# The first value projection of a bidirectional hybrid layer, computed from the scaled input before its norm and shift are known

## The chip, the cores and the metric

The kernel runs on one core of a Trainium2 chip. The metric is the device time of one execution in microseconds; the kernel before took 2884.38 us (median of 3 runs, 2880.95 to 2885.03). One execution was recorded with the hardware profiler. Lower is better.

The names of the engines in the rows: PE is the matrix engine (TensorE), DVE is VectorE, ACT is ScalarE, POOL is GpSimd, and SP is the engine whose queue issues most of the DMA transfers.

## The reference

One layer of a backbone is applied to 640 tokens of width D = 2048: 128 context tokens (a prompt with its own conditioning vector) and 512 latent tokens (a sample with another). What matters here is its beginning:

```python
def rmsnorm(x, g):
    y = xf * lax.rsqrt(jnp.mean(xf * xf, -1, keepdims=True) + EPS)
    return (y * g.astype(jnp.float32)).astype(x.dtype)
...
    sh1, sc1, g1, sh2, sc2, g2 = modulation(cond, p['w_mod'], p['b_mod'])   # silu(cond) @ w_mod + b_mod
    u = rmsnorm(x, p['g_pre_mix']) * (1.0 + sc1) + sh1
    mix, new_state = mixer(u, rows, state, p)
...
    q, k, v, o, ig, fg, z, xbc, dt = jnp.split(u @ p['w_in'], _split_points(IN_SIZES), axis=-1)
```

So every projection of the mixer multiplies u by a part of w_in. Per token t, u = x · r(t) · a + sh, where r(t) is the reciprocal root mean square of the token's row, a = g_pre_mix · (1 + sc1) and sh = sh1. The vectors a and sh have one value per feature and conditioning vector (2 of them), and come from two 2048-wide column groups of the matrix w_mod. The value projection v has 1024 columns, the gates (ig, fg, dt) have 48. Behind the projections stand the mLSTM and SSD recurrences, the output projection and the MLP, which make up most of the time and are the same in both kernels.

## The kernel before

**Tiles.** Features lie on the 128 partitions: x is loaded transposed as `xT`, 16 k-tiles of 128 features by 640 tokens. The left and right factors of the precise products are split in two float32r parts: `ah` and `al` hold the high and the low part of u for the 16 k-tiles, `whi` and `wlo` those of a weight block (`split_block`: ACT rounds the block to `whi`, DVE subtracts). Each product is the sum of three matmuls, high·high, low·high and high·low (`mm_a` with the weights stationary, `mm_b` with the tokens stationary).

**The first stage** (lines 295 to 378), which the change rewrites:

- All of `xT` is loaded first (8 transfers, 2 k-tiles each). ACT squares each k-tile; DVE adds the squares up; 25 matmuls with a column of ones (line 317) sum over the features; the power -0.5 is taken on POOL (line 320); five matmuls with a matrix of ones (line 329) spread r(t) over the partitions as `rb`.
- `mod1(k)` computes a and sh of k-tile k. It streams four 512 KB blocks of w_mod (two transfers) and runs 16 float32 matmuls of 32 x 256 (line 346), four at a time in the four 32-column groups of PE. ACT copies the sums out (line 350, `part`), two transposes (line 261, `mod1t`) turn them, and DVE reduces them and writes `a1` and `modT` (lines 262, 354, 355).
- For each k, DVE and ACT build u (line 366), `ah` (line 367) and `al` (line 368), and PE multiplies it: six matmuls into the gates' two PSUM banks `gps` (line 220), and for each second k 30 matmuls into the five banks `vps` of the first 512 columns of v, "chunk v0" (lines 236 to 238).

**Behind it**, ACT copies the gates out (line 429), ACT and DVE copy the five banks of v0 into a value tile (`v_tile`, line 421), and PE goes on with the transposes of the gates (line 437), a step of the later modulation (`mod_step`, line 272: four float32 matmuls) and chunk v1 (`proj_b`). The gates' own long chain on DVE then runs beside v1 and the first query and key projections.

**What sets the order.** The kernel is written as nested calls; a scheduler places the instructions of each engine in a fixed queue, by a simulated timeline, and a pool's number of buffers decides when a load may be issued. All weight and input loads stand in the one queue of SP, which issues in order: a load that waits for its buffer holds those behind it. The weights lie in HBM in the order in which `block_keys` lists them.

## Time and profile before

| | us |
|---|---|
| three timed runs | 2880.95, 2884.38, 2885.03 |
| the profiled execution, its own time | 2880.88 |
| its span in the trace | 2879.2 |
| PE busy | 2829.3 (98%) |
| DVE busy | 1939.3 (67%) |
| ACT busy | 1287.2 (45%) |
| POOL busy | 408.6 (14%) |

The profiled execution took 1.7 us more than its span, and lies at the lower end of the three timed runs. PE's busy time is modelled from pipelined matmuls: each matmul's record overlaps that of the next one, so what a matmul takes in a row of many is read from the distance between two starts, not from the mean duration of one. A float32 matmul has two records, a float32r matmul one. PE's granted clock was 0.998 of full speed over the span. The busy shares are means over the whole layer; the change lies in the first 150 us, so the rows below are from there, except for a few prices that only later stages show.

### The profile page before, as it was taken

How to read it: one execution, taken by the hardware profiler on the slowest of the kernel's cores; microseconds unless marked ns; L12 is line 12 of the kernel's file. 1: busy time of each engine (PE TensorE's matmuls, PEld its weight loads, DVE VectorE, ACT ScalarE, POOL GpSimd, SP SyncE). 2: the span in 40 equal slices, each digit the busy share in tenths (PEclk: the TensorE clock that was granted, in tenths of full speed). 3: DMA queues.
4: the chain of work that ended last, by engine and by line, in shares of the span. 5: the costliest groups of instructions: out<-in, count | busy, mean ns of one | idle time of the engine just before them, and what ended most of it. 6: DMA issues, size and time to landing. Idle time of an engine off the chain costs nothing.

```text
span 2879.2 us, 48401 instructions
## 1 busy us (share of the span) xinstructions
PE 2829.3 (98%) x18882; PEld 2631.5 (91%) x18882; DVE 1939.3 (67%) x3121; ACT 1287.2 (45%) x2315; POOL 408.6 (14%) x454
## 2 busy tenths in 40 slices
PE   7999999999999999999999999999999999999998
PEld 5679898888887889998999999999999999999997
DVE  4463465787665757678777666666776676677976
ACT  3222333334413433565444444444565566465364
POOL 0000000223211000000000000000014444443200
PEclk9999999999999999999999999999999999999999
DMA  9743434555647667655444333333448998998254
GB/s 366 288 141 108 138 126 138 176 167 156 210 139 227 233 241 253 215 193 166 161 154 138 116 110 113 109 109 108 163 129 182 207 210 190 197 210 185 89 199 167
DMA packets 211748, 498.52 MB, mean 173 GB/s; under 512 B 22424, under 2 KB 111768, under 8 KB 211008
## 3 DMA queue, kind: packets, MB, share of 16 engines
q1 hardware_dynamic: 153872, 429.38, 43.8%
q0 software_dynamic: 39792, 45.73, 10.0%
q10 hardware_dynamic: 17856, 20.32, 1.9%
q8 instruction: 148, 2.42, 0.3%
q14 instruction: 80, 0.66, 0.1%
HBM read 405.33 MB, written 44.97 MB: 156 GB/s over the span
## 4 chain that ended last, share of the span: by engine, by line
PE 86%; DVE 4%; issue 3%; DMA 3%; POOL 2%; ACT 1%; SPq 0%; DVEq 0%; POOLq 0%; ACTq 0%
PE mm L837 18%; PE mm L835 18%; PE mm L836 18%; PE mm L220 10%; PE mm L236 3%; PE mm L238 3%; PE mm L237 3%; PE tr L272 3%; POOL pc L1244 2%; DVE wlo L963 1%; PE mod L346 1%; PE vps L236 1%; DMA raw<-in_w 1%; PE vps L237 1%; PE vps L238 1%
## 5 line engine op out<-in xcount | busy, mean ns | idle before, releaser
L963 ACT CAST whi<-raw 128x512 fp32r<-128x512 f32 (+1 forms) x659 | 499.1, 766 | 588.4 <-PE mm L836 381.1
L963 DVE TENSOR_TENSOR wlo<-raw,whi 128x512 fp32r<-128x512 f32 (+1 forms) x659 | 574.3, 881 | 248.0 <-ACT whi L963 243.9
L835 PE MATMUL mm<-ah,whi 128*128 128x320 f32 x1536 | 478.4, 312 | 8.3 <-ACT whi L963 8.3
L836 PE MATMUL mm<-al,whi 128*128 128x320 f32 x1536 | 475.7, 310 | 0.0
L837 PE MATMUL mm<-ah,wlo 128*128 128x320 f32 x1536 | 474.6, 310 | 1.0 <-DVE wlo L963 0.6
L207 ACT CAST whi<-raw 128x1024 fp32r<-128x1024 f32 x162 | 169.4, 1047 | 422.4 <-PE mm L238 131.1
L835 PEld LDWEIGHTS mm<-ah,whi 128*128 128x128 f32 x1536 | 288.6, 188 | 18.0 <-ACT whi L963 9.8
L208 DVE TENSOR_TENSOR wlo<-raw,whi 128x1024 fp32r<-128x1024 f32 x162 | 202.2, 1249 | 142.1 <-ACT whi L207 141.1
L837 PEld LDWEIGHTS mm<-ah,wlo 128*128 128x128 f32 x1536 | 288.1, 188 | 6.4 <-issue 4.1
L836 PEld LDWEIGHTS mm<-al,whi 128*128 128x128 f32 x1536 | 288.7, 188 | 4.2 <-issue 4.1
L1244 POOL DMA_DIRECT2D pc<-ev x275 | 238.4, 896 | 368.2 <-ACT ev L1243 357.4
L220 PE MATMUL mm<-ah,whi 128*128 128x256 f32 (+1 forms) x768 | 189.7, 319 | 0.0
L220 PE MATMUL mm<-al,whi 128*128 128x256 f32 (+1 forms) x768 | 188.9, 318 | 0.0
L220 PE MATMUL mm<-ah,wlo 128*128 128x384 f32 (+1 forms) x768 | 185.9, 316 | 0.0
L236 PE MATMUL mm<-whi,ah 128*128 128x512 f32 x400 | 161.7, 405 | 0.0
L238 PE MATMUL mm<-whi,al 128*128 128x512 f32 x400 | 159.6, 399 | 0.0
L237 PE MATMUL mm<-wlo,ah 128*128 128x512 f32 x400 | 159.4, 399 | 0.0
L837 PE MATMUL mm<-q,wlo 128*128 128x320 f32 x512 | 157.9, 308 | 0.0
L835 PE MATMUL mm<-q,whi 128*128 128x320 f32 x512 | 157.9, 308 | 0.0
L1243 ACT COPY ev<-mm 128x320 f32<-128x320 f32 x275 | 115.7, 425 | 63.2 <-DMA pc<-ev 45.3
L220 PEld LDWEIGHTS mm<-ah,whi 128*128 128x128 f32 x768 | 121.1, 188 | 10.2 <-issue 9.1
L220 PEld LDWEIGHTS mm<-ah,wlo 128*128 128x128 f32 x768 | 120.7, 188 | 6.9 <-issue 5.8
(424 smaller groups left out, 6680.2 us busy)
## 6 DMA issues: line engine op xcount, KB each, us to landing
raw<-in_w SPq DMA_DIRECT2D x460, 512.0 KB, 3.4
mraw<-in_w SPq DMA_DIRECT2D x128, 512.0 KB, 4.3
pc<-ev POOLq DMA_DIRECT2D x275, 160.0 KB, 5.3
m<-in_w SPq DMA_DIRECT2D x32, 1024.0 KB, 6.6
R<-hd SPq DMA_DIRECT2D x32, 640.0 KB, 6.2
xs<-csd SPq DMA_DIRECT2D x40, 256.0 KB, 5.4
hd<-s ACTq DMA_DIRECT2D x62, 160.0 KB, 3.3
hd<-u ACTq DMA_DIRECT2D x62, 160.0 KB, 1.9
```

Source lines behind the costliest of these rows:

```text
L207: S.copy(hi, t)
L208: V.tensor_sub(lo, t, hi)
L220: PE.matmul(ps[h][:, 0:HW[h]], lhsT=w[:, cs_], rhs=a[:, k, HS[h]], start=(k == 0 and i == 0), stop=(k == KT - 1 and i == 2))
L236: PE.matmul(ps[:, :], lhsT=ah[:, k, tok], rhs=hi[:, wc], start=first, stop=False)
L237: PE.matmul(ps[:, :], lhsT=ah[:, k, tok], rhs=lo[:, wc], start=False, stop=False)
L238: PE.matmul(ps[:, :], lhsT=al[:, k, tok], rhs=hi[:, wc], start=False, stop=last)
L835: PE.matmul(ps, lhsT=wh[:, c], rhs=bh[:, k, :], start=(start and k == 0), stop=False)
L836: PE.matmul(ps, lhsT=wh[:, c], rhs=bl[:, k, :], start=False, stop=False)
L837: PE.matmul(ps, lhsT=wl[:, c], rhs=bh[:, k, :], start=False, stop=(stop and k == nk - 1))
L963: newest[:] = S.copy(hi, src), V.tensor_sub(lo, src, hi)
L1243: S.copy(ev, ps)
L1244: G.dma_start(pi[:, j, :], ev, accum_op=OP.add)
```

## The change

Chunk v0 no longer waits for the norm. Since u = x·a·r(t) + sh, v0 is r(t) · (x·a) W + sh W, where W is the block of w_in; the change computes the two parts apart.

- **From scaled x.** `scaled(k)` writes ah and al of x·a (ACT multiplies by a, DVE subtracts), without r(t) and sh; chunk v0's matmuls run on these. After they have used a k-tile, `modulated(k)` replaces it by u as before, for all later projections. `MD` says after which pair p of k-tiles which pairs are replaced; the first four k-tiles after p = 3 and p = 4, the last four after p = 7.
- **The norm at PSUM's exit.** `v_tile` multiplies each bank by rc5 (r of the bank's tokens) and adds the shift's part, in one DVE instruction a bank.
- **The shift's part.** For each k-tile one float32 matmul (line 408) multiplies sh, two values a feature in a 32-wide tile `shT`, by the raw block of 512 columns, each k in one of four 32-column groups of one bank `vsh`; they are written four together after each second pair. At the end ACT copies the bank out, two matmuls with a selecting matrix (line 477) add the four groups and spread the sums over the partitions, and ACT copies them out.
- **The norm** is computed in the middle (`first_norm`, after pair 2): five matmuls for the sums over features instead of 25, then as before.
- **Loads.** x's eight loads are spread over pairs 0 to 2 (`XL`). mod1's blocks are single 512 KB transfers in seven buffers (five of their own and the two of `mraw`), where before four 1 MB tiles were used. The raw blocks of v0 have three buffers in place of two and are kept until the shift's matmul has read them.
- **The gates** are no longer computed within the loop but as an ordinary projection (`proj_a("g", 0)`, 96 matmuls) behind chunk v0 and ahead of chunk v1.

The core of the diff:

```diff
-            for k in range(KT):
-                if k % 2 == 0:
-                    SY.dma_start(xT[:, k:k + 2, :], A["xT"][:, k * T:(k + 2) * T].rearrange("p (a b) -> p a b", b=T))
...
-            def load_m1(k):
-                    w = p0.tile([P, 2, 1024], F32, tag="m1", name="m1", bufs=4)
...
             def mod1(k):
+                for j in range(4):
+                    i = more["m1"] = more.get("m1", -1) + 1
+                    if i % 7 < 2:
+                        w = wp.tile([P, 1024], F32, tag="mraw", name="mraw", bufs=2)
+                    else:
+                        w = p0.tile([P, 1024], F32, tag="m1", name="m1", bufs=5)
+                    SY.dma_start(w, A["w"][BLK["m1", k, j]])
...
+                V.tensor_copy(shT[:, k, 0:2], modT[:, k, :])
...
+            def scaled(k):
+                for ci, cc in enumerate(CC):
+                    S.activation(ah[:, k, cc], xT[:, k, cc], AF.Copy, scale=a1[:, k, ci:ci + 1])
+                    V.scalar_tensor_tensor(al[:, k, cc], xT[:, k, cc], a1[:, k, ci:ci + 1], ah[:, k, cc],
+                                           OP.mult, OP.subtract)
...
-                mm_a(gps, k, gw[0], gw[1])
...
+            XL = {0: (1, 2), 1: (3, 4, 5), 2: (6, 7)}
+            MD = {3: (0,), 4: (1,), 5: (2, 3), 6: (4, 5), 7: (6, 7)}
+            raws = {}
+            for p in range(KT // 2):
+                raws[p] = raw_block(("B", "v", 0, p))
+                vw = split_block(None, raws[p])
+                if p == 0:
+                    mod1(1)
+                for i in XL.get(p, ()):
+                    load_x(i)
+                if p + 1 < KT // 2:
+                    mod1(2 * p + 2)
+                    mod1(2 * p + 3)
+                for k in (2 * p, 2 * p + 1):
+                    scaled(k)
+                for i in ((0,) if p == 0 else ()) + XL.get(p, ()):
+                    squares(i)
                 for kk in range(2):
+                    k = 2 * p + kk
                     for t in range(NT):
-                        mm_b(vps[t], t, k - 1 + kk, vw[0], vw[1], kk, k - 1 + kk == 0, k - 1 + kk == KT - 1)
+                        mm_b(vps[t], t, k, vw[0], vw[1], kk, k == 0, k == KT - 1)
+                if p % 2:
+                    for g in range(4):
+                        k = 2 * p - 2 + g
+                        PE.matmul(vsh[32 * g:32 * g + 32, :], lhsT=shT[:, k, :],
+                                  rhs=raws[k // 2][:, k % 2 * 512:(k % 2 + 1) * 512], start=(p == 1), stop=(p == 7))
+                if p == 2:
+                    first_norm()
+                for i in MD.get(p, ()):
+                    for k in (2 * i, 2 * i + 1):
+                        modulated(k)
...
+                if shift:
+                    V.scalar_tensor_tensor(o, i, rc5[:, t:t + 1],
+                                           shift[t > 0][:, 0:512].rearrange("p (h e) -> p h e", h=2), OP.mult, OP.add)
...
+        part, shift = fmt(), []
+        S.copy(part[:, 0:512], vsh)
+        for c in range(2):
+            sel = gp.tile([P, P], F32, tag="vsel", name="vsel", bufs=2)
+            V.tensor_scalar(sel, ones, vcol[:, c:c + 1], None, OP.mult)
+            ps = pva()
+            PE.matmul(ps, lhsT=sel, rhs=part[:, 0:512], start=True, stop=True)
+            shift.append(fmt())
+            S.copy(shift[c][:, 0:512], ps)
+        vts = [v_tile(vps, shift)]
...
+        for i, ps in enumerate(proj_a("g", 0)):
+            S.copy(gT[:, HS[i]], ps[0:48, 0:HW[i]])
```

How the change moves instructions on the engines is shown at three places. `m1`, `m` and `mraw` are blocks of w_mod for mod1, `raw` are blocks of w_in; the numbers behind `m` and `part` are buffers, in order of use.

The queue of SP at the start of the program, before:

```order
L111 DMA par<-in_par 128x377
L113 DMA row<-in_row 128x96
L303 DMA xT<-in_xT 128x1280 x8
L337 DMA m_213<-in_w 128x2x1024
L337 DMA m_215<-in_w 128x2x1024
L337 DMA m_243<-in_w 128x2x1024
L337 DMA m_245<-in_w 128x2x1024
```

The same place in the changed program, from its first block of w_mod on:

```order
L323 DMA mraw<-in_w 128x1024 x2
L323 DMA m_120<-in_w 128x1024
L323 DMA m_122<-in_w 128x1024
L340 DMA xT<-in_xT 128x1280
L199 DMA raw<-in_w 128x1024
L323 DMA m_164<-in_w 128x1024
L323 DMA m_166<-in_w 128x1024
L323 DMA m_168<-in_w 128x1024
L323 DMA mraw<-in_w 128x1024
L340 DMA xT<-in_xT 128x1280 x2
```

The blocks of the first k-tile now come ahead of x, and the eight transfers of x stand among blocks of w_mod and w_in: the last of them, x's k-tiles 14 and 15, has 11 blocks of w_mod, 3 of w_in and the 7 other transfers of x ahead of it.

PE in the middle of the loop, before, from one mod1's transposes to the next product of the gates:

```order
L261 MATMUL mod1t<-ident,part_392 128x128 x2
L346 MATMUL mod_418<-m_414,scT 32x256 x8
L236 MATMUL vps<-whi,ah 128x512
L237 MATMUL vps<-wlo,ah 128x512
L346 MATMUL mod_418<-m_416,scT 32x256 x8
L238 MATMUL vps<-whi,al 128x512
L220 MATMUL gps<-ah,whi 128x384
L220 MATMUL gps<-ah,whi 128x256
```

PE in the middle of the loop of the changed program, from the last high products of one k-tile of v0 to mod1 of the next but one:

```order
L235 MATMUL vps<-whi,ah 128x512
L236 MATMUL vps<-wlo,ah 128x512
L408 MATMUL vsh<-raw,shT 32x512
L237 MATMUL vps<-whi,al 128x512 x5
L260 MATMUL mod1t<-ident,part_645 128x128 x2
L328 MATMUL mod_663<-mraw,scT 32x256 x4
L328 MATMUL mod_663<-m_657,scT 32x256 x4
L328 MATMUL mod_663<-m_659,scT 32x256 x4
L328 MATMUL mod_663<-m_661,scT 32x256 x4
```

The gates' matmuls have left the loop. The shift's matmuls, written four together in the source, stand one by one, one in each k-tile's stretch, with float32r matmuls of the full width on both sides; mod1's 16 matmuls stand together behind the transposes.

ACT behind chunk v0 in the changed program (`fm` are scratch tiles; the cast in the third row is of a block of chunk v1):

```order
L374 ACTIVATE ah<-u,modT 128x128
L374 ACTIVATE ah<-u,modT 128x512
L206 CAST whi<-raw 128x1024
L472 COPY fm<-vsh 128x512
L514 ACTIVATE arow<-row 128x32
L479 COPY fm<-pva 128x512 x2
L206 CAST whi<-raw 128x1024 x2
```

PE at the same place:

```order
L237 MATMUL vps<-whi,al 128x512 x5
L477 MATMUL pva<-fm,vsel 128x512 x2
L271 MATMUL tr<-mraw,scT 32x256 x4
L219 MATMUL mm<-ah,whi 128x384
L219 MATMUL mm<-ah,whi 128x256
```

Before, the gates' copies (line 429) and the copies of the five banks stood at this place of ACT, and on PE the gates' transposes followed v0's last matmuls directly. Now the shift's copy stands behind a cast that needs the buffer of v0's last weight block, PE's two selecting matmuls wait for that copy, and the gates' 96 matmuls come between v0 and v1.

## Rows read from the trace of the kernel before

**Rows 1.** The page: span, PE's busy time and the engines' shares of the chain of waits.

```profile
span 2879.2 us, 48401 instructions
...
PE 2829.3 (98%) x18882; PEld 2631.5 (91%) x18882; DVE 1939.3 (67%) x3121; ACT 1287.2 (45%) x2315; POOL 408.6 (14%) x454
...
PE 86%; DVE 4%; issue 3%; DMA 3%; POOL 2%; ACT 1%; SPq 0%; DVEq 0%; POOLq 0%; ACTq 0%
```

**Rows 2.** Busy time of the engines in stretches of 20 us: stretch, length, PE, PEld, DVE, ACT, POOL (busy us and number of instructions), PE's granted clock, busy share of the DMA engines, GB/s.

```profile
0.00:20.00 20.00, 2.62 (x12) 2.57 (x12) 10.45 (x21) 12.32 (x18) 1.20 (x8) 1.00 0.87 332
20.00:40.00 20.00, 19.73 (x133) 15.87 (x133) 6.07 (x14) 4.89 (x10) 1.18 (x1) 1.00 1.00 394
40.00:60.00 20.00, 19.32 (x159) 12.34 (x158) 10.03 (x23) 6.36 (x11) 0.00 (x0) 1.00 1.01 397
...
120.00:140.00 20.00, 18.69 (x168) 12.33 (x165) 9.77 (x23) 6.89 (x12) 0.00 (x0) 1.00 0.53 194
...
160.00:180.00 20.00, 20.00 (x103) 14.77 (x101) 11.03 (x31) 3.16 (x6) 0.00 (x0) 1.00 0.38 133
```

**Rows 3.** For whom PE waited in the first 150 us: who, for whom, total us, times, longest.

```profile
PE nrm L317 <- ACT sq L305: 15.6, 1, 15.6
PE mod L346 <- DVE sm L262: 2.6, 9, 0.5
...
PE ms L437 <- ACT v L421: 1.0, 1, 1.0
```

**Rows 4.** PE's timeline from the start: start, length, line, operation, tiles, count of records, idle before.

```profile
17.94 4.42 PE L317 MATMUL nrm<-ones,sq 128*128 128x1 f32 x20 [15.57 <-ACT sq L305]
22.23 2.27 PE L317 MATMUL nrm<-ones,rb 128*128 128x1 f32 x10
24.36 4.41 PE L317 MATMUL nrm<-ones,sq 128*128 128x1 f32 x20
28.69 3.64 PE L346 MATMUL mod<-m,scT 128*32 128x256 f32 x32
32.26 2.40 PE L329 MATMUL nrm<-rb,ones 128*128 128x128 f32 x10
34.50 0.38 PE L261 MATMUL mod1t<-ident,part 128*128 128x128 f32 x2
35.15 1.93 PE L346 MATMUL mod<-m,scT 128*32 128x256 f32 x32 [0.27 <-DVE sm L262]
37.02 0.50 PE L236 MATMUL vps<-whi,ah 128*128 128x512 f32 x1
```

**Rows 5.** PE's timeline in the loop: one k-tile from transposes to transposes.

```profile
48.45 0.38 PE L261 MATMUL mod1t<-ident,part 128*128 128x128 f32 x2
...
55.92 0.38 PE L261 MATMUL mod1t<-ident,part 128*128 128x128 f32 x2
56.56 1.07 PE L346 MATMUL mod<-m,scT 128*32 128x256 f32 x16 [0.27 <-DVE sm L262]
...
63.35 0.38 PE L261 MATMUL mod1t<-ident,part 128*128 128x128 f32 x2
```

**Rows 6.** PE's timeline behind the first stage: the last product of v0, the gates' transposes, a mod_step, and chunk v1's first products up to the next mod_step.

```profile
146.53 1.09 PE L238 MATMUL vps<-whi,al 128*128 128x512 f32 x4
148.66 0.51 PE L437 MATMUL ms<-ident,fm 48*128 48x48 f32 x5 [1.04 <-ACT v L421]
149.10 0.64 PE L272 MATMUL tr<-mraw,scT 128*32 128x256 f32 x8
149.67 0.50 PE L236 MATMUL mm<-whi,ah 128*128 128x512 f32 x1
150.01 0.40 PE L237 MATMUL mm<-wlo,ah 128*128 128x512 f32 x1
...
156.75 0.64 PE L272 MATMUL tr<-mraw,scT 128*32 128x256 f32 x8
```

**Rows 7.** PE's timeline in a later stage: two float32 matmuls of 257 columns between float32r matmuls.

```profile
282.02 0.60 PE L658 MATMUL ms<-St,qw 128*128 128x257 f32 x2
282.45 0.60 PE L659 MATMUL ms<-v,pT 128*128 128x257 f32 x2
282.70 0.65 PE L220 MATMUL mm<-ah,wlo 128*128 128x384 f32 x2
```

**Rows 8.** The chain of waits, in order of time (start, length, what): 48 matmuls of a projection of the gates' form, one weight block.

```profile
223.22 7.08 PE mm L220 x48
```

**Rows 9.** ACT's timeline: the squares of x's first and last transfer, each started when the transfer had landed.

```profile
7.61 0.74 ACT L305 ACTIVATE rb<-xT 128x640 f32<-128x640 f32 x1 [4.11 <-DMA xT<-in_xT]
...
18.73 1.36 ACT L305 ACTIVATE sq<-xT 128x640 f32<-128x640 f32 x2 [0.22 <-DMA xT<-in_xT]
```

**Rows 10.** Groups of instructions of DVE and ACT in the first 152 us: line, engine, operation, tiles and shapes, count, busy us, mean ns of one, idle before.

```profile
L368 DVE SCALAR_TENSOR_TENSOR al<-u,modT,ah 128x512 fp32r<-128x512 f32 x16 | 12.0, 750 | 5.8 <-ACT ah L367 5.8
...
L309 DVE TENSOR_TENSOR rb<-rb,sq 128x640 f32<-128x640 f32 x11 | 9.1, 825 | 6.1 <-ACT sq L305 5.0
...
L421 DVE COPY v<-vps 128x512 f32<-128x512 f32 x2 | 1.2, 647 | 0.0
...
L207 ACT CAST whi<-raw 128x1024 fp32r<-128x1024 f32 x13 | 13.6, 1043 | 25.4 <-PE vps L238 20.4 <-PE gps L220 5.0
...
L421 ACT COPY v<-vps 128x512 f32<-128x512 f32 x3 | 1.7, 587 | 0.1
```

More of the change, by code (lines that the diff above doesn't have):

```diff
@@ L311, in build @@
-            pt = pv.tile([P, 512], F32, tag="g", name="nrm", bufs=2)
-            parts = [late[KT - 4], late[KT - 3], rb, late[KT - 2], late[KT - 1]]
-            V.memset(rc5, 0.0)
-            PE.matmul(pt[:, 0:NT], lhsT=ident, rhs=rc5, start=True, stop=False)
-            for n, x in enumerate(parts):
-                for i in range(NT):
-                    PE.matmul(pt[:, i:i + 1], lhsT=x[:, i * P:(i + 1) * P], rhs=ones[:, 0:1],
-                              start=False, stop=n == 4 and i == NT - 1)
@@ L332, in load_m1 @@
[L332 to L342 removed]
+            shT = p0.tile([P, KT, 32], F32, name="shT")
+            V.memset(shT, 0.0)
@@ new lines, in load_x, with squares, first_norm @@
+            def load_x(p):
+                SY.dma_start(xT[:, 2 * p:2 * p + 2, :],
+                             A["xT"][:, 2 * p * T:(2 * p + 2) * T].rearrange("p (a b) -> p a b", b=T))
+            def squares(p):
+                for k in (2 * p, 2 * p + 1):
+                    sq = tmp("sq") if k else rb
+                    S.activation(sq, xT[:, k, :], AF.Square)
+                    if k:
+                        V.tensor_add(rb, rb, sq)
+            def first_norm():
+                pt = pva()
+                for i in range(NT):
+                    PE.matmul(pt[:, i:i + 1], lhsT=rb[:, i * P:(i + 1) * P], rhs=ones[:, 0:1], start=True, stop=True)
+                V.tensor_scalar(rc5, pt[:, 0:NT], 1.0 / D, EPS, OP.mult, OP.add)
+                G.tensor_tensor(rc5, rc5, mhalf[:, 0:NT], OP.pow)
+                for i in range(NT):
+                    V.tensor_scalar(rb[:, i * P:(i + 1) * P], ident, rc5[:, i:i + 1], None, OP.mult)
+                for c in (slice(0, 512), slice(512, T)):
+                    pt = pva()
+                    for i in range(c.start, c.stop, P):
+                        PE.matmul(pt[:, i - c.start:i - c.start + P], lhsT=ones, rhs=rb[:, i:i + P], start=True, stop=True)
+                    S.copy(rb[:, c], pt[:, 0:c.stop - c.start])
```

84 lines of the change are left out of this document (30 added, 54 removed).

## The prediction

> **What bounds the kernel now.** I read the page first: PE is busy for 2829.3 of 2879.2 us and takes 86% of the chain of waits [rows 1]. So a stage gains only what PE is spared in it, and what PE loses is not made up later: from 160 us on PE is busy 20.00 us in 20 [rows 2]. Next, the stretches of the first stage. In the first 20 us PE works 2.6 us while the loads run at 332 GB/s; from 20 to 60 us both are full (PE 19.3 to 19.7 of 20, DMA share 1.00, 394 to 397 GB/s); towards the end the loads fall to 0.53 and PE stays at 18.7 [rows 2]. So before, the stage is bound by the load of x at its head and by PE behind it, with the loads close below. The waits say the same: PE's one long wait is 15.6 us for the squares of x; all others together are 5 us [rows 3]. On the timeline that head has three parts: nothing until 17.94, then 25 slow norm matmuls until 28.69 (10.75 us, 0.43 each), then mod1 [rows 4].
>
> The mark by which I measure is the start of chunk v1 on PE: 149.67 us before, with the gates done and five gate transposes (148.66 to 149.10, 0.44 us) and one mod_step (0.57 us) ahead of it [rows 6].
>
> **The start of the changed program: when PE stops waiting for loads.** x arrives at (18.73 - 7.61) / 7 = 1.59 us for each 655,360 bytes [rows 9]; a block of 524,288 bytes then takes 0.8 of that, 1.27 us, and the stream begins at 7.61 - 1.59 = 6.0 us. The changed queue of SP puts 11 blocks of w_mod, 3 of w_in and 7 other transfers ahead of x's last. It lands at 6.0 + 14 x 1.27 + 8 x 1.59 = 36.5 us, where before the last landed at 18.7. Until then PE can do mod1 of k-tiles 0 to 2 and v0 of k-tiles 0 and 1, some 14 us of work in 30: it starves, because x stands in the way of w_mod. Then come two squares (1.36 us, rows 9), an addition of 0.83 us [rows 10] and five norm matmuls (5 x 0.43 = 2.2 us, rows 4). PE's queue holds the transposes of k-tile 2 behind those, so they run at about 41.1 us. Before, they ran at 48.45 [rows 5], with the same v0 work and two k-tiles of the gates done. So the twenty norm matmuls saved (8.6 us) and the early start leave a lead of 7 us here, not of 28.
>
> **The loop from there, for PE.** One k-tile's stretch in the changed order is: transposes and the wait for DVE's reduction until mod1 may take the bank, 0.64 us [rows 5]; mod1's 16 matmuls together, 35.15 to 37.02, 1.87 us [rows 4]; 15 matmuls of v0, by the spacing of v1's 30 (149.67 to 156.75, 0.236 each, rows 6), 3.54 us; and one matmul of the shift.
>
> The shift's matmul is the new price. The nearest rows are two float32 matmuls of 257 columns between float32r ones: the second starts 0.43 us after the first [rows 7]. For 512 columns that makes 0.86. Its weights are 32 columns wide, as in a mod_step, where four of 256 columns take 0.57 us [rows 6] against 0.43 for one, so the change to 32-column groups and back costs 0.14: in all 1.0 us. The upper bound is 1.14 (twice the mod_step). The lower bound is 0.25: mod1's sixteen take 1.87 us, 0.117 for each 256 columns because four run at once, and an alone-standing one would cost that little only if it ran beside its neighbours. I take 1.0, since in the order it stands between matmuls of full width, as in rows 7.
>
> The Trainium skill's page "TensorE: Matmul & The Clock Gate", section "Part 3: Packing small matmuls — row/col tiling", says that matmuls at different column positions run at the same time, so that a pack costs little more than one of them. This case's trace agrees where four stand together: 0.57 us for four of 256 columns. By that rule the source's four matmuls of the shift would cost about 1.0 us together, 0.25 each; the scheduled order has taken the pack apart, and the sum below does not use it.
>
> The sum is 0.64 + 1.87 + 3.54 + 1.0 = 7.05 us. Read the other way: before, the 14 k-tiles from 48.45 to the end of v0 at 147.62 took 7.08 each, gates of 0.88 us included (a sixteenth of two times 7.08, rows 8); with 1.0 in their place that is 7.20. I take 7.1. The loads need 4.5 blocks x 1.27 = 5.7 us for a k-tile, so they keep up. DVE gains one more pair of instructions for each k-tile (0.75 us for the 512 columns, rows 10, and less for the 128) on top of 10 us in 20 [rows 2]: hidden. ACT's share is smaller still.
>
> So the transposes of k-tile 15 run at 41.1 + 13 x 7.1 = 133.4, plus 2.4 us for the norm's five spreading matmuls [rows 4] and 0.6 for a mod1 that the order splits: 136.4. The last k-tile has no mod1 to hide its chain: 2.5 us from transposes to first product (34.50 to 37.02, rows 4), 3.54 and 1.0: v0 ends at 143.5. Before it ended at 147.62.
>
> **Behind v0.** Before, PE waited 1.04 us for the copies [rows 3]. Now a chain of ACT and PE stands there, with nothing else on PE: the cast that is queued ahead of the shift's copy and needs v0's last weight tile (1.04 us, rows 10), the copy (0.59), a selecting matmul (0.87, from rows 7), its copy (0.59), the second matmul in the same single bank (0.87) and its copy (0.59): 4.55, and 0.1 for each handover, 5.1 us. Queued behind the waiting matmul are the mod_step and all gates. It could be as short as 2.5 us, if the cast and the second round are out of the way, and as long as 7. DVE's five instructions at PSUM's exit (0.65 us each as copies, rows 10) run beside the gates; only the first bank's is waited for. Then a mod_step (0.57) and the gates, two weight blocks of 7.08 us [rows 8], 14.2: chunk v1 starts at 143.5 + 5.1 + 14.7 = 163.3. The gates' transposes (0.44), already done before at this mark, come later: 163.8 against 149.67, which is 14.1 us later. The gates leave the loop and come back whole, so they cancel; the delay is the shift's matmuls, the chain behind v0 and the starved start, less the lead of 7 us.
>
> Behind the mark PE's work is the same and PE is full, so the delay stays. The gates' chain starts one block of v1 later; v1 and the first queries cover it as before.
>
> **The number.** The sum is made on the profiled execution: 2880.88 + 14.1 = 2895.0. That execution lies 3.5 us under the median of the runs, which spread over 4.1. I add the 14 to the middle of the three runs, 2883.0: 2897 us. 0.2% of the time, 5.8 us, is about what a measurement can tell from no change.
>
> **Rivals.**
> - *The shift's matmuls run beside their neighbours.* At 0.25 us each, 14 of them in the stretch that PE bounds give 10.5 us back: +3.6, 2887, not to be told from no change. For it speaks the packing of mod1's matmuls; against it that the neighbours use all 128 columns. Chance 0.12.
> - *The early start pays.* PE's 18 idle and 10.75 slow us at the head are real, and the last block of w_mod could land at 6.0 + 72 x 1.27 + 8 x 1.59 = 110 us. If PE followed the loads, v0 would end at about 110 + 1.1 + 7.1 = 118, v1 start at 138.5: -11, 2872. The place is the loop: it decides from a stretch under 7.1 - 14.1 / 13 = 6.0 us on. Against it: the matmuls alone are 6.4. Chance 0.07.
> - *The order of loads holds PE up.* The raw blocks now wait for the shift's matmul of three pairs ago, and blocks of w_mod stand behind them in SP's queue. The shift's matmul ends some 8 us before the next stretch but one begins, and PE needs the block behind it only in that stretch; two blocks land in 3 to 6 us. Should it fail, each of the last four pairs costs about 3 us: +26, 2909. Chance 0.12.
> - The forecast, with its own range of 2890 to 2904: 0.62. What is left, 0.07, is a later stage that the scheduler has rearranged, to either side.
>
> Faster than by 0.2% holds the early start: 0.07. Within 0.2%: the rival of the packed matmuls, 0.12. Slower: 0.81. The range of 2885 to 2910 takes in the bounds of the shift's matmul and of the chain behind v0 and the held-up loads; it leaves the early start out.
>
> **What the profile will show.** First product of v0 before 20 us, but PE under half busy until 40; x's last squares at 36 to 38 us. A period of 7.1 us between two pairs of transposes, with one line 408 matmul after which the next starts 0.9 to 1.1 us later. A gap on PE of 3 to 4 us around the line 477 matmuls near 145 us, ended by ACT. Gates of 14 us, v1 from about 163. I am wrong if the period is near 6, if line 408 takes 0.3 us, or if the delay at v1's start is not that at the end.

## The result, and the profile after

The changed kernel takes 2922.23 us (median of 4 runs, 2919.06 to 2924.19), the kernel before 2884.31 (4 runs, 2880.95 to 2885.03): a ratio of 1.0132, 95% interval 1.0118 to 1.0146, or 38 us more. The forecast was 2897 in a range of 2885 to 2910. Its direction held; its size was too small by 25 us and the range did not hold the time. The profiled execution of the changed kernel took 2920.77 us, that of the kernel before 2880.88, which lies 3.4 us under the median of its runs; so a lag that is read between the two traces ends 2 us above the difference of the medians.

The page after, against [rows 1]:

```profile
span 2919.0 us, 48592 instructions
...
PE 2856.4 (98%) x18876; PEld 2630.1 (90%) x18876; DVE 1959.5 (67%) x3180; ACT 1300.9 (45%) x2346; POOL 411.1 (14%) x454
...
PE 87%; DVE 6%; DMA 4%; issue 2%; ACT 1%; POOL 0%; SPq 0%; DVEq 0%; ACTq 0%; POOLq 0%
```

PE has six records fewer and is busy 27 us longer. The stretches of the first stage after, against [rows 2] (the last three columns are PE's granted clock, DMA share and GB/s):

```profile
0.00:20.00 20.00, 10.09 (x49) 3.20 (x49) 5.51 (x19) 5.16 (x8) 1.20 (x8) 1.00 0.87 321
20.00:40.00 20.00, 14.19 (x86) 6.68 (x85) 15.05 (x22) 13.11 (x20) 0.00 (x0) 0.86 1.02 411
40.00:60.00 20.00, 19.27 (x120) 11.74 (x121) 10.69 (x32) 7.53 (x16) 1.18 (x1) 0.80 0.87 321
120.00:140.00 20.00, 17.66 (x123) 9.85 (x125) 8.61 (x26) 5.80 (x12) 0.00 (x0) 1.00 0.69 252
140.00:160.00 20.00, 15.19 (x80) 7.33 (x70) 14.40 (x36) 9.21 (x16) 1.45 (x2) 0.93 0.38 123
160.00:180.00 20.00, 19.80 (x126) 17.71 (x123) 6.20 (x10) 2.73 (x4) 0.00 (x0) 0.89 0.38 119
```

PE starts earlier and is then emptier: 24.3 us of work in the first 40, against 22.4 before. In four of the six stretches the granted clock is under 1.00, where it reads 1.00 in all of [rows 2]. At the head that reading cannot be taken at its word: up to 34.5 us the kernel before ran its matmuls at half their later pace (mod1's 16 took 32.26 - 28.69 = 3.57 us, and 1.87 from 35.15 on, rows 4), and so did the changed kernel up to about 21 us (eight records of mod1 take 0.94 us from 20.03 on and 0.46 from 23.49 on). The waits of PE up to 160 us, against [rows 3]:

```profile
PE mod L328 <- DVE sm L261: 9.4, 14, 0.8
PE mod L328 <- DMA mraw<-in_w: 7.9, 1, 7.9
PE mod L328 <- DMA m<-in_w: 4.3, 3, 3.9
PE vps L235 <- ACT ah L366: 2.5, 2, 1.7
PE pva L477 <- ACT fm L472: 1.7, 1, 1.7
...
PE pva L477 <- ACT fm L479: 0.7, 1, 0.7
PE tr L271 <- ACT fm L479: 0.7, 1, 0.7
```

The first line is the surprise: 2.6 us in 9 times before, now 9.4 in 14, up to 0.8 each. PE's head, against [rows 4]:

```profile
33.65 1.07 PE L328 MATMUL mod<-m,scT 128*32 128x256 f32 x16
38.58 1.08 PE L328 MATMUL mod<-m,scT 128*32 128x256 f32 x8 [3.87 <-DMA m<-in_w]
40.20 2.29 PE L353 MATMUL pva<-ones,rb 128*128 128x1 f32 x10 [0.53 <-DVE rb L348]
42.35 0.67 PE L260 MATMUL mod1t<-ident,part 128*128 128x128 f32 x2
```

One k-tile of the loop on PE, against [rows 5], and DVE beside it:

```profile
105.11 1.04 PE L408 MATMUL vsh<-raw,shT 128*32 128x512 f32 x2
106.09 1.42 PE L237 MATMUL vps<-whi,al 128*128 128x512 f32 x5
107.34 0.38 PE L260 MATMUL mod1t<-ident,part 128*128 128x128 f32 x2
108.50 1.93 PE L328 MATMUL mod<-m,scT 128*32 128x256 f32 x32 [0.78 <-DVE sm L261]
110.37 0.50 PE L235 MATMUL vps<-whi,ah 128*128 128x512 f32 x1
...
115.13 0.38 PE L260 MATMUL mod1t<-ident,part 128*128 128x128 f32 x2
```

```profile
106.69 0.35 DVE L375 SCALAR_TENSOR_TENSOR al<-u,modT,ah 128x128 fp32r<-128x128 f32 x1 [3.66 <-PE vps L237]
107.61 0.75 DVE L375 SCALAR_TENSOR_TENSOR al<-u,modT,ah 128x512 fp32r<-128x512 f32 x1 [0.57 <-PE vps L237]
108.28 0.17 DVE L261 TENSOR_REDUCE sm<-mod1t 128x4 f32<-128x16 f32 x1
```

The period is 115.13 - 107.34 = 7.79 us. The shift's matmul takes 106.09 - 105.11 = 0.98 of it. The reduction `sm`, for which PE's next mod1 waits, stands in DVE's queue behind the low part of a replaced k-tile (line 375), and that waits for PE's last product of the k-tile (line 237). So mod1's matmuls wait 0.78 us behind the transposes, half a microsecond more than the 0.27 of before. Behind v0, against [rows 6]:

```profile
151.99 1.32 PE L237 MATMUL vps<-whi,al 128*128 128x512 f32 x5
155.04 1.13 PE L477 MATMUL pva<-fm,vsel 128*128 128x512 f32 x2 [1.72 <-ACT fm L472]
156.84 1.58 PE L477 MATMUL pva<-fm,vsel 128*128 128x512 f32 x2 [0.68 <-ACT fm L479]
159.09 1.08 PE L271 MATMUL tr<-mraw,scT 128*32 128x256 f32 x8 [0.68 <-ACT fm L479]
...
177.03 0.64 PE L271 MATMUL tr<-mraw,scT 128*32 128x256 f32 x8
177.60 0.50 PE L235 MATMUL mm<-whi,ah 128*128 128x512 f32 x1
```

Chunk v1 starts at 177.60 against 149.67: 27.9 us later. The remaining 10 us of the 38 come behind that mark, in stages that the change does not touch. By the first state matmul of the mLSTM (257.9 before) the lag is 30.8, at the last MLP matmul of line 888 it is 39.9, the 2 us named above included. The granted clock is not the cause there: from v1 to the end it reads 1.00 in both traces.

### The profile page after: what moved, and what is told of

The parts are those of the page before. It is cut to its first block, busy times and chain, and to the rows that moved or that the text cites. A ratio compares the mean times of both kernels' runs of the same rounds, so it can differ in the third digit from the quotient of the medians.

```text
span 2919.0 us, 48592 instructions
## 1 busy us (share of the span) xinstructions
PE 2856.4 (98%) x18876; PEld 2630.1 (90%) x18876; DVE 1959.5 (67%) x3180; ACT 1300.9 (45%) x2346; POOL 411.1 (14%) x454
## 4 chain that ended last, share of the span: by engine, by line
PE 87%; DVE 6%; DMA 4%; issue 2%; ACT 1%; POOL 0%; SPq 0%; DVEq 0%; ACTq 0%; POOLq 0%
PE mm L888 19%; PE mm L890 19%; PE mm L889 19%; PE mm L219 10%; PE mm L235 3%; PE mm L237 3%; PE mm L236 3%; PE tr L271 2%; DMA raw<-in_w 2%; DMA R<-hd 1%; DVE wlo L1016 1%; PE mod L328 1%; DMA xs<-csd 1%; PE vps L235 1%; PE vps L237 1%
## 5 line engine op out<-in xcount | busy, mean ns | idle before, releaser
L888 PEld LDWEIGHTS mm<-ah,whi 128*128 128x128 f32 x1536 | 289.0, 188 | 19.4 <-ACT whi L1016 10.0
L890 PEld LDWEIGHTS mm<-ah,wlo 128*128 128x128 f32 x1536 | 288.4, 188 | 5.7 <-issue 3.7
L889 PEld LDWEIGHTS mm<-al,whi 128*128 128x128 f32 x1536 | 289.0, 188 | 3.0 <-issue 2.9
L219 PE MATMUL mm<-ah,whi 128*128 128x384 f32 (+1 forms) x800 | 199.1, 322 | 0.2 <-DVE v L461 0.2
L219 PE MATMUL mm<-al,whi 128*128 128x384 f32 (+1 forms) x800 | 196.0, 319 | 0.0
L219 PE MATMUL mm<-ah,wlo 128*128 128x384 f32 (+1 forms) x800 | 193.7, 317 | 0.0
L219 PEld LDWEIGHTS mm<-ah,whi 128*128 128x128 f32 x800 | 127.2, 190 | 10.8 <-issue 9.6
L219 PEld LDWEIGHTS mm<-al,whi 128*128 128x128 f32 x800 | 126.8, 190 | 7.4 <-issue 6.2
```

Of the source, the lines that this page charges most:

```text
L219: PE.matmul(ps[h][:, 0:HW[h]], lhsT=w[:, cs_], rhs=a[:, k, HS[h]], start=(k == 0 and i == 0), stop=(k == KT - 1 and i == 2))
L888: PE.matmul(ps, lhsT=wh[:, c], rhs=bh[:, k, :], start=(start and k == 0), stop=False)
L889: PE.matmul(ps, lhsT=wh[:, c], rhs=bl[:, k, :], start=False, stop=False)
L890: PE.matmul(ps, lhsT=wl[:, c], rhs=bh[:, k, :], start=False, stop=(stop and k == nk - 1))
```

## The experiments

18 kernels ran. For each, the table gives the median, the ratio to the kernel before with its interval, the difference to the kernel before run beside it (its medians were 2883.2 to 2885.8), the lag of v1's first matmul in the trace, and the rest, which came behind that mark. The lag is that of one trace, and the first stage alone differs by 1 to 2 us between executions (e12 and e17 start v1 earlier than the kernel before with the same instructions). The last column, a difference of medians less the lag of a trace, is therefore good to some 3 us. The trace of the kernel before is late at v1 and early at the end, so a lag that is read to the end of a trace grows more: by 7.0 us behind v1 in e14, a plain delay, and by 12.0 in the changed kernel. Differences from the changed kernel below are of the medians; with the kernel before of the same run as base they are up to 1.2 us smaller.

| | median us | ratio (95%) | over before | v1's lag | behind v1 |
|---|---|---|---|---|---|
| changed kernel | 2922.2 | 1.0132 (1.0118-1.0146) | 37.9 | 27.9 | 10.0 |
| e1 12 shift matmuls out | 2905.3 | 1.0081 (1.0068-1.0095) | 22.2 | 13.7 | 8.5 |
| e2 shift matmuls together | 2903.5 | 1.0074 (1.0061-1.0088) | 20.3 | 11.0 | 9.3 |
| e3 DVE's order | 2914.1 | 1.0113 (1.0099-1.0126) | 30.9 | 21.2 | 9.7 |
| e4 before, gates later | 2903.7 | 1.0069 (1.0056-1.0081) | 20.5 | 10.6 | 9.9 |
| e5 e4 without two mod_steps | 2899.1 | 1.0050 (1.0037-1.0063) | 14.8 | 10.5 | 4.3 |
| e6 e2 and e3 | 2902.0 | 1.0062 (1.0049-1.0075) | 17.7 | 12.6 | 5.1 |
| e7 x's loads spread | 2913.5 | 1.0102 (1.0086-1.0117) | 29.2 | 18.9 | 10.3 |
| e8 all of these | 2909.7 | 1.0089 (1.0075-1.0103) | 25.4 | 15.1 | 10.3 |
| e9 without two mod_steps | 2924.4 | 1.0133 (1.0119-1.0146) | 38.6 | 27.9 | 10.7 |
| e10 e2 without mod_steps, two banks | 2907.6 | 1.0078 (1.0063-1.0094) | 21.8 | 10.8 | 11.0 |
| e11 filler | 2923.8 | 1.0132 (1.0115-1.0150) | 38.0 | 27.9 | 10.1 |
| e12 before, 64 bytes | 2888.5 | 1.0014 (1.0005-1.0023) | 3.6 | -1.8 | 5.4 |
| e13 e5, 64 bytes | 2905.1 | 1.0073 (1.0061-1.0086) | 20.2 | 9.6 | 10.6 |
| e14 before, plain delay | 2897.8 | 1.0045 (1.0032-1.0059) | 12.9 | 9.9 | 3.0 |
| e15 old places | 2919.5 | 1.0118 (1.0103-1.0133) | 35.7 | 29.4 | 6.3 |
| e16 old places, no mod_steps | 2924.2 | 1.0133 (1.0119-1.0147) | 40.3 | 30.6 | 9.7 |
| e17 before, 32 bytes lower | 2896.6 | 1.0033 (1.0021-1.0046) | 12.7 | -1.2 | 13.9 |
| e18 e16 with e2 | 2902.4 | 1.0058 (1.0045-1.0070) | 18.5 | 11.4 | 7.1 |

None is faster than the kernel before.

**The loop: e1, e2, e3, e6.** e1 leaves out the shift's matmuls of k-tiles 4 to 15 and keeps the first four:

```diff
-                if p % 2:
+                if p == 1:
...
-                                  rhs=raws[k // 2][:, k % 2 * 512:(k % 2 + 1) * 512], start=(p == 1), stop=(p == 7))
+                                  rhs=raws[k // 2][:, k % 2 * 512:(k % 2 + 1) * 512], start=True, stop=True)
```

> The changed kernel with 12 of its 16 shift matmuls left out (only those of k-tiles 0 to 3 stay, so the shift's part of the first value chunk is incomplete). Theory (each shift matmul costs PE about 1.0 us of its own, as the spacing in the changed kernel's loop says): the 12 cost 12 us, chunk v1 starts near 165.5 instead of 177.6, the period between two pairs of transposes is 6.8 instead of 7.78 us, and the time is about 2910. Rival (the period is set by another chain, DVE's or the loads', and the shift's matmuls lie in its slack): the period stays above 7.5, v1 starts after 174, the time is 2918 to 2922.

16.9 us faster than the changed kernel; v1 starts 14.3 earlier (163.32), and the period from k-tile 4 to 15 is 6.6 us in the mean, between 5.5 and 7.2. The rival falls: the matmuls cost 14.3 / 12 = 1.2 us each, together with what they hold up (PE's waits for `sm` fall from 9.4 to 5.9 us). e2 queues the four behind the pair's last product:

```diff
-                        mm_b(vps[t], t, k, vw[0], vw[1], kk, k == 0, k == KT - 1)
+                        last = mm_b(vps[t], t, k, vw[0], vw[1], kk, k == 0, k == KT - 1)
...
+                        with tc.issue_after(last.ins):
+                            PE.matmul(vsh[32 * g:32 * g + 32, :], lhsT=shT[:, k, :],
```

> The changed kernel with the four shift matmuls of two pairs kept together behind the pair's last product. Theory (standing alone is what makes them dear: four in the four column groups run at once, as mod1's do): four take 1.0 to 1.2 us together instead of 4 x 1.0, about 11 us less at the start of v1, time about 2911. Rival (a float32 matmul of 512 columns costs its 1.0 us wherever it stands): no difference, 2922. Second rival (the raw blocks are now held until the end of the pair, and w_mod blocks queue behind the next one): PE waits for loads, 2922 or more with DMA waits in the loop.

PE's timeline of e2, the four (8 records) and what follows:

```profile
111.26 1.06 PE L409 MATMUL vsh<-raw,shT 128*32 128x512 f32 x8
112.25 0.44 PE L260 MATMUL mod1t<-ident,part 128*128 128x128 f32 x2
```

Four take 112.25 - 111.26 = 0.99 us, as long as one alone in the changed kernel. That is what the Trainium skill's page "TensorE: Matmul & The Clock Gate", section "Part 3: Packing small matmuls — row/col tiling", says of matmuls at different column positions, here shown for 512 columns. The gain was 18.7 us and not 11, 16.9 of it at v1. Of that, 12 x 0.98 = 11.8 us are the matmuls, and 2.7 are waits: only 9 of the k-tiles still waited for DVE (6.7 us in all), not 14 (9.4). The other 2.4 are not taken apart. e3 changes DVE's queue alone:

```diff
+                    with tc.issue_after(done[min(k + 1, KT - 1)].ins):
                         V.scalar_tensor_tensor(al[:, k, cc], u[:, cc], modT[:, k, ci:ci + 1], ah[:, k, cc],
```

> The changed kernel with the low part of each replaced k-tile queued on DVE behind the low part of the next scaled k-tile, so that it no longer stands between PE's last product and the reduction of mod1's sums. Theory (DVE's queue holds the reduction behind an instruction that waits for PE itself, 0.5 us for each k-tile from k-tile 4 on): the wait of mod1's matmuls falls from 0.78 to 0.27 us, the period from 7.78 to 7.3, v1 starts 5 to 6 us earlier and the time is about 2916. Rival (something else is late next, ACT or the w_mod blocks): the period stays at 7.7 or more, 2922.

```profile
104.66 0.38 PE L260 MATMUL mod1t<-ident,part 128*128 128x128 f32 x2
105.30 1.93 PE L328 MATMUL mod<-m,scT 128*32 128x256 f32 x32 [0.27 <-DVE sm L261]
...
111.93 0.38 PE L260 MATMUL mod1t<-ident,part 128*128 128x128 f32 x2
```

In this timeline of PE the wait is 0.27 and the period 111.93 - 104.66 = 7.27, as expected; the time is 8.2 us under the changed kernel's. So the half microsecond is DVE's queue.

e6 has the edits of e2 and e3.

> The changed kernel with both: the four shift matmuls together (e2) and the low parts of replaced k-tiles behind the scaled ones on DVE (e3). Theory (two separate losses): e2's period of 6.73 us loses the 0.5 us on those k-tiles where DVE's reduction still stood behind, about 6 us in all, v1 starts near 155 and the time is 2896 to 2899. Rival (the packing took that loss away already, since e2 gained 18.7 us and not 11): 2902 to 2904.

The rival holds: e6 is no faster than e2 (2902.0 and 2903.5), and v1 starts 1.6 us later in it. With the matmuls together, PE waits 6.7 us for the reduction, with DVE's order changed as well 7.3: this order on DVE takes nothing off those waits once the matmuls stand together. Why they remain is not shown.

**The head: e7 and e11.** e7 queues x's loads behind the w_mod blocks and spreads them:

```diff
+                    with tc.issue_after(mdma[2 * p + 2].ins):
+                        for i in XL.get(p, ()):
+                            load_x(i)
...
-            XL = {0: (1, 2), 1: (3, 4, 5), 2: (6, 7)}
-            MD = {3: (0,), 4: (1,), 5: (2, 3), 6: (4, 5), 7: (6, 7)}
+            XL = {0: (1,), 1: (2, 3), 2: (4, 5), 3: (6, 7)}
+            MD = {4: (0, 1), 5: (2, 3), 6: (4, 5), 7: (6, 7)}
```

> The changed kernel with x's loads held behind the w_mod blocks of their pair in SP's queue and spread over pairs 0 to 3, the norm after pair 4 and the replacing from pair 4 on. Theory (the changed kernel starves at its head because the scheduler puts seven x loads ahead of the w_mod blocks of k-tiles 2 and 3): the wait of 7.9 and 4.3 us for w_mod goes, the granted clock stays at full in 20 to 60 us, the transposes of k-tile 2 run near 33 instead of 42.4, the period stays 7.8, v1 starts 7 to 9 us earlier, time 2913 to 2915. Rival (the loads are only moved: the same bytes are missing two or three pairs later): k-tile 2 near 33 but k-tile 9 where it was, time 2920 to 2923. A second one: the replaced k-tiles come so late that the gates wait for DVE, 2922 or more.

The first stretches of e7:

```profile
20.00:40.00 20.00, 17.82 (x128) 9.23 (x126) 9.06 (x17) 7.58 (x12) 0.00 (x0) 1.00 1.03 410
40.00:60.00 20.00, 17.93 (x128) 9.83 (x128) 9.52 (x24) 8.56 (x15) 0.00 (x0) 1.00 1.03 410
```

The transposes of k-tile 2 run at 31.38 instead of 42.35, the clock stays at full, v1 starts 9.0 us earlier and the time is 8.7 lower. The theory holds for the sum, but not for the way there: the lead over the changed kernel is 13.6 us at k-tile 3, 8.5 at k-tile 9 (a period of 8 to 9 us where x's loads and the norm now stand), and 9.9 at k-tile 15.

e11 fills the wait of 3.87 us ahead of k-tile 2's transposes:

```diff
+                    if k == 2 and kk == 12:
+                        dummy = pva()
+                        for _ in range(4):
+                            with tc.issue_after(m.ins):
+                                m = PE.matmul(dummy, lhsT=ones, rhs=xT[:, 0, 0:512], start=True, stop=True)
```

> The changed kernel with four extra float32 matmuls of 512 columns, whose result nobody reads, in PE's queue where it waits 3.9 us for the last w_mod block of k-tile 2 (34.7 to 38.6 us). Theory (the granted clock falls to half behind that wait, and the work until 48.7 us pays for it): with the wait filled the clock stays at full in 38 to 49, k-tile 3's transposes run 2.5 to 4 us earlier than at 53.15, the time is 2918 to 2920. Rival (the clock there costs nothing, since the stretch waits for loads and DVE anyway, or falls all the same): k-tile 3 within 1 us of 53.15, or later by what the extra work costs; 2922 or more.

The granted clock in the changed kernel, in stretches of 2 to 3 us, and then in e11:

```profile
35.00:38.00 3.00, 0.00 (x0) 0.00 (x0) 2.89 (x4) 2.18 (x5) 0.00 (x0) 0.99 1.01 405
38.00:40.00 2.00, 1.08 (x8) 0.20 (x8) 1.79 (x3) 0.99 (x3) 0.00 (x0) 0.50 1.05 418
...
46.00:48.00 2.00, 2.00 (x7) 0.34 (x3) 1.23 (x1) 0.08 (x1) 0.00 (x0) 0.50 1.03 410
48.00:50.00 2.00, 2.00 (x17) 1.29 (x16) 0.00 (x0) 0.00 (x0) 0.00 (x0) 0.96 1.03 410
```

```profile
35.00:38.00 3.00, 1.86 (x5) 0.56 (x3) 2.79 (x3) 2.28 (x4) 0.00 (x0) 1.00 1.02 407
38.00:40.00 2.00, 1.14 (x11) 0.42 (x11) 1.75 (x4) 0.82 (x2) 0.00 (x0) 1.00 1.03 410
...
42.00:44.00 2.00, 2.00 (x4) 0.50 (x2) 1.42 (x6) 0.00 (x0) 0.72 (x1) 0.50 1.04 408
44.00:46.00 2.00, 2.00 (x13) 0.77 (x12) 0.23 (x1) 1.05 (x1) 0.00 (x0) 0.73 1.02 410
```

Between the theories: the stretch at the lower level (1.2 of 2.4 GHz) shrank from ten microseconds to about three and a half, but did not go; k-tile 3's transposes came 2.6 us earlier (50.57; the last block of k-tile 2 was there 0.3 earlier) and k-tile 15's 2.4. Yet v0's last products ran at 151.91, in the changed kernel at 151.99, and the time is the same. PE's timeline of e11 in the last k-tile of v0:

```profile
146.74 0.50 PE L235 MATMUL vps<-whi,ah 128*128 128x512 f32 x1 [2.53 <-ACT ah L372]
...
147.39 1.87 PE L414 MATMUL vsh<-raw,shT 128*32 128x512 f32 x2
149.19 0.80 PE L235 MATMUL vps<-whi,ah 128*128 128x512 f32 x1
```

That k-tile waited 2.5 us for ACT instead of 1.7, and behind the wait the granted clock fell again, to 0.51 from 147.5 to 151 us: the shift's matmul took 149.19 - 147.39 = 1.80 us instead of 0.98. So the clock's price at the head was real, and filling the wait won nothing: what it gave was lost at v0's end, to ACT's `ah` and to the clock.

**The gates: e4, e5, e9.** e4 is the kernel before with this one part of the change: no `mm_a` in the loop, the gates' blocks listed behind v0's, and `proj_a("g", 0)` behind v0 in place of the two copies.

> The kernel before with one part of the change alone: the gates out of the loop, as an ordinary projection behind chunk v0. Theory (the gates' matmuls only move, and what comes behind is the same): v1 starts within 2 us of 149.67 plus the two mod_steps that now stand ahead of it (1.1 us), time 2884 to 2887. Rival (the gates' chain, now one block of v1 later, puts the mLSTM and SSD stages in another order that costs the 10 to 12 us which the changed kernel loses behind v1's start): v1 near 150, but the end 8 to 14 us later, 2893 to 2898.

Both theories miss: 20.5 us. v1 starts 10.6 us later, where I had expected 3 at most. The two blocks of gates are back, 14 us, and two mod_steps; but the loop without them gained only 4.3 by v0's last products (142.27 against 146.53). Its last two k-tiles took (137.53 - 123.85) / 2 = 6.84 us each, against (140.94 - 127.22) / 2 = 6.86 before. Where the gates' products had stood, PE now waits more: 4.0 us for the reduction (before 2.6) and 2.4 for `ah` (before none). That is 3.8 of the 9.9 us that the loop did not give back; the rest I cannot place. And 10 us more came behind v1. e5 leaves the two mod_steps out of the gates' projection:

```diff
-                if mod["n"] < MODCAP[0]:
+                if name != "g" and mod["n"] < MODCAP[0]:
```

> The run with the gates moved alone (e4), but without the two mod_steps that the gates' projection issues as every projection does, so that each later mod_step stands at the block where it stood before. Theory (e4 loses 10 us behind its first mLSTM instructions because every later mod_step comes two blocks earlier and the scheduler arranges the SSD and MLP stages otherwise): the lag against the kernel before stays at 10 to 12 us from the first mLSTM instruction to the end, time 2892 to 2895. Rival (the gates' chain that arrives later does it): the lag grows by 8 to 11 us as in e4, time 2901 to 2905.

2899.1: behind v1 4.3 us are left of 9.9, although PE now waits 1.6 us for v0's banks (in e4 0.9) and 2.1 for v1's behind v1. The intervals of e4 and e5 overlap (1.0056 to 1.0081 and 1.0037 to 1.0063), so the difference is hardly clear of noise. It looked like the theory; e9 is the same edit in the changed kernel.

> The changed kernel without the two mod_steps in the gates' projection, nothing else. Theory (those two steps shift all later ones by two blocks, and the other arrangement of the SSD and MLP stages costs 6 to 9 us, as e4 against e5): v1 starts about 1 us earlier, the lag against the kernel before stays flat from the first mLSTM instruction (near 31) to the end instead of growing by 9 us, time 2913 to 2916. Rival (in the changed kernel the growth comes from its other loads or its longer delay): the lag still ends at 38 to 40, 2920 to 2923.

It fell: 2924.4, with 10.7 us behind v1. From v1 on e9's order on PE is that of e5 but for 46 of 17,074 matmuls. The same order grows by 4 us in one and by 11 in the other.

**Put together: e8, e10.** e8 has e2, e3, e5's edit, e7's and, for the second selecting matmul, a bank of its own; e10 has e2, e5's edit and that bank.

> The changed kernel with all of it: shift matmuls together, DVE's order, x's loads spread (e7), no mod_steps in the gates' projection, and a bank of its own for the second selecting matmul behind v0. Theory (separate losses): 2922 - 18.7 - 5 - 9 - 8 - 1 is 2880, at or below the kernel before. Rival (the losses overlap: each of them hides another, since PE has one queue): 2890 to 2897.

> The changed kernel with the shift matmuls together (e2), no mod_steps in the gates' projection and a second bank for the second selecting matmul. Theory (the losses add here, since they stand in different stretches): 2903.5 - 7 - 1 is 2895 to 2896. Rival (e8's way: arranging one stage anew spoils another): 2902 or more.

e10's rival holds; e8 is slower than even its rival had it (2890 to 2897), so the losses overlap by more than I thought. In e8 PE waits 4.9 us for ACT's `part` and 4.3 for `ah` in the loop, where squares, norm and replaced k-tiles now all stand, behind v0 2.2 us for the shift's last copy and 1.7 for v0's banks, and 1.9 for v1's banks behind v1. e10's six runs spread from 2902.8 to 2914.7, more than any other kernel's.

**Behind v1: e14, e12, e13, e17, e15, e16, e18.** e14 puts 14 unread float32 matmuls into the last k-tile of v0, in the kernel before.

> The kernel before with 14 float32 matmuls of 512 columns, whose result nobody reads, on PE within the last k-tile of chunk v0: a plain delay of 14 x 0.86 = 12 us ahead of v1. Theory (what comes behind v1 only moves): 12 us at v1 and 12 at the end, 2895 to 2898. Rival (any delay of the first stage costs more behind, because the scheduler arranges later stages anew): 12 at v1, 17 to 22 at the end, 2902 to 2906.

12.9 us, as the theory says: the 14 matmuls hold PE for 11.2 us (142.83 to 151.01 and 152.30 to 155.33), v1 starts 9.9 later, since the wait of 1.0 us for v0's banks is gone and the trace is 0.8 quicker up to k-tile 15's transposes. So a plain delay moves what follows and costs 2 or 3 us more at the end. e12 is the kernel before with 64 bytes more of constants; every instruction's place in its queue is the same, one memset aside. The changed kernel has this shift too: `rc5` and `vcol` stand among the constants.

```diff
+        padt = cp.tile([P, 16], F32, name="padt")
+        V.memset(padt, 0.0)
```

> The kernel before with one unused tile of 64 bytes a partition behind its constants, so that every later tile lies 64 bytes higher, as in the changed kernel; no engine's order of instructions differs from the kernel before, apart from one memset. Theory (the drift behind v1's start, which the same order has in e9 and not in e5, comes from where the tiles lie): 6 to 10 us slower, 2890 to 2895. Rival (place has no price): within 3 us of the kernel before.

> e5 (gates later, without their two mod_steps) with the same 64 bytes. Its order behind v1 is e9's but for 46 of 17,074 places, and now its addresses are e9's too. Theory (place): the lag grows behind the first mLSTM instruction by 8 to 11 us as in e9, time 2904 to 2908. Rival (the arrival of data behind the changed first stage): as e5, 2897 to 2901.

> The kernel before with one constant tile of 32 bytes laid into a tile that is no longer used: the weight tiles now begin at multiples of 256 bytes (before: 32 above one; in the changed kernel 96 above one); the order stays. Theory (it is the alignment of the tiles that has a price): 2 to 5 us faster than before, 2880 to 2882. Rival (any other place is worse or as good by chance): 2884 to 2889.

e12 is 3.6 us slower (ratio 1.0005 to 1.0023), between its theory and its rival; e13 is 5.4 slower than e5 against the kernel before, with 10.6 us behind v1 as in e9. e17, 32 bytes lower with every tile of weights at a multiple of 256 bytes, is slower by 12.7 (9.5 by the ratio), more than either of its theories has: place has a price, and it is not alignment in this sense. Where it is paid is harder to say. PE's groups of e17 over the whole program, then those of the kernel before, and then those of e14, whose tiles lie where they lay before (count, busy us, mean ns of one, idle ahead):

```profile
L835 PE MATMUL mm<-ah,whi 128*128 128x320 f32 x1536 | 479.6, 312 | 8.2 <-ACT whi L963 8.2
...
L236 PE MATMUL mm<-whi,ah 128*128 128x512 f32 x400 | 162.7, 407 | 0.0
```

```profile
L835 PE MATMUL mm<-ah,whi 128*128 128x320 f32 x1536 | 478.4, 312 | 8.3 <-ACT whi L963 8.3
...
L236 PE MATMUL mm<-whi,ah 128*128 128x512 f32 x400 | 161.7, 405 | 0.0
```

```profile
L840 PE MATMUL mm<-ah,whi 128*128 128x320 f32 x1536 | 479.4, 312 | 10.3 <-ACT whi L968 10.3
...
L236 PE MATMUL mm<-whi,ah 128*128 128x512 f32 x400 | 161.7, 405 | 0.0
```

e17 is about 1 us longer than the kernel before in each large group of matmuls, 0.3 to 0.8%, and waits 4 us more for DVE's `wlo` in the MLP (7.9 against 3.8). But e14's first group is as long as e17's without any tile having moved, so that part is not the place; the groups of 512 columns and the waits (in e14 3.8 as before) may be. The lag of e17 grows little by little through mLSTM, SSD and the MLP's end, and not at all between 1350 and 2030 us; e14's grows in the same way, by 7.0 us.

e15 lays `rc5` and `vcol` into a constant that is no longer used, in the changed kernel; e16 adds e5's edit, e18 e2 too.

```diff
-        rc5 = cp.tile([P, NT], F32, name="rc5")
+        rc5 = cth[:, 0:NT]
```

> The changed kernel with its two new small constants (rc5, vcol) laid into a constant tile that is no longer used, so that every later tile lies where it lay before the change, 64 bytes lower; the order on all engines stays. Theory (place, as e12's 3.6 and e13's 5.4 us more): 4 to 5 us faster than the changed kernel, 2917 to 2919. Rival (place matters only with before's order): 2921 to 2924.

> e15 and no mod_steps in the gates' projection: the changed first stage, with the order behind v1 and the addresses of e5. Theory (growth behind v1 is place plus order, about 5 us each): the lag grows by 4 us as in e5 instead of 10, time 2915 to 2918 (v1 starts at +28). Rival (a third cause in the changed kernel): the lag grows by 8 or more, 2920 or later.

> The changed kernel with the shift matmuls together, the tiles at their old places and no mod_steps in the gates' projection. Theory (separate causes add): v1 at +11 as in e2, 4 us of growth behind it, 2899 to 2900, the fastest with the changed first stage. Rival (as e10, where the other arrangement spoiled it): 2903 or more.

e15 is 2.7 us faster, less than its runs spread (2914 to 2924): not told apart. e16 has e5's order and places, but 9.7 us behind v1 and not 4: the rival, something in the changed first stage itself, holds, and I cannot name it. e18 is no faster than e2 or e6; only its profiled execution, the lowest of its five, grows by 4.9 us behind v1 as its theory has it.

## Why the prediction was wrong

By its steps, first to v1's start (forecast 163.3, measured 177.6):

- *What bounds the kernel* held, and so did "what PE loses is not made up later".
- *The start* was right in kind: k-tile 2's transposes at 42.35, forecast 41.1. PE starved because x stood ahead of w_mod; e7 gave 9 us back. That the granted clock would fall to half behind such a wait was not in the sum; e11 puts its price at about 2.4 us, which k-tile 15's transposes still show and v0's end no longer does. With the norm matmuls the sum was lucky: its 0.43 us for one comes from the slow head of the kernel before, and in the changed kernel the five ran at the lower level too (2.15 us together, 42.35 - 40.20); in e11, at 0.92 to 1.00 of the clock, they take 1.21.
- *The shift's matmul*: 0.98 us to the next one's start, forecast 1.0 in all; the borders below come on top. Its rival (beside its neighbours) is dead by e1 and e2.
- *"DVE gains one more pair of instructions ...: hidden"* is the step that failed in the loop. I counted DVE's busy time (10 us in 20) and not its queue: a low part that waits for PE stands ahead of the reduction that PE waits for. 0.5 us in each k-tile from k-tile 4 on (e3), 5.6 in eleven. The rest of 7.78 - 7.1 is some 0.2 us at the borders between float32 and float32r matmuls, one behind mod1's and two beside the shift's: ten products take 2.52 and five 1.26, where 0.236 each makes 2.36 and 1.18. From k-tile 2 to 15 it came to 103.9 us, forecast 95.3: 8.6 more.
- *Behind v0* the chain was near: 153.3 (last product and its length) to the mod_step at 159.09 is 5.8, forecast 5.1. *"Then a mod_step (0.57) and the gates"* was short by two mod_steps of 0.57, which `proj_a` issues with each block, and by the gates' first products at half clock (0.53 us a pair until 164, later 0.29): 18.5 in place of 14.7.
- *"The gates leave the loop and come back whole, so they cancel"* is wrong as a sentence. My stretch was built from its parts, so the sum did not use it, but e4 shows that this part alone costs 10.6 us at v1, of which 3.8 are waits that the gates' products had filled.

1.3 + 8.6 + 0.7 + 3.8 makes 14.4, the 14.3 at that mark. The other 10 us are the step *"behind the mark PE's work is the same and PE is full, so the delay stays"*. As a statement on a delay it holds to 2 or 3 us (e14). As a statement on this change it failed: 10 us behind v1 here, 3 to 14 in the variants; against e14, a delay alone, the changed kernel loses 7 us more by the medians and 5 by the traces. The prediction had named a delay at the end other than that at v1 as a sign of being wrong. Shown is that the place of the tiles, which the change shifts by 64 bytes, is worth 3.6 us with the order of before and 5.4 with e5's. That the mod_steps' order is worth 5.7 at the places of before (e4 against e5) is not shown: the intervals overlap, and the same edit gains nothing in the changed kernel (e9) nor at the old places (e16 against e15). How the changed kernel's 10 divide stays open: e15 and e16, which take away the place and then both, do not bring them back.

The other rivals: the early start did not pay (period 7.8, not under 6.0); the order of loads did not hold PE up in the loop (all its waits for w_mod lie before 39 us). The remainder of 0.07 for a rearranged later stage was too small. Two readings were off without weight in the sum: PE's other waits in the 150 us of [rows 3] make 6.8 us (2.6, 1.8, 1.4 and 1.0) and not 5, and PE was busy for 24.3 of the first 40 us, not under half.

## What to carry to other kernels

An engine that is half idle hides added work only if nothing in its queue waits for the engine that waits for it: look at what stands ahead of the awaited instruction, not at busy time. Work in a loop may fill a wait there, so moving it out is not neutral; time the loop without it. And when later stages drift with the same order of instructions, time the old kernel with its tiles moved by some bytes, and with a plain delay, before looking for a mechanism.

## What the runs showed that was not expected

- Moving the weight tiles by 64 bytes up or 32 down, with the same instructions in the same order, cost 3.6 and 9 to 13 us of 2884. Where the loss is paid and by what rule is open.
- After PE had stood idle from 35 to 38 us, its granted clock was 0.50 of full from 38 to 48 us, though it was busy for most of these; spread loads (e7) kept it at 1.00 from 20 to 60 us.
- Four float32 matmuls of 32 x 512 in the four column groups take 0.99 us together, one between full-width matmuls 0.98 to the next one's start.
